# Attention scores and GLA state products on all 128 rows and columns of TensorE

## The chip, the cores and the metric

The kernel runs on one core of a Trainium2 chip. A core has TensorE (PE in the profile: matrix products into PSUM, with a load of the stationary operand, PEld, for each), VectorE (DVE), ScalarE (ACT), GpSimd (POOL) and SyncE (SP), and 16 DMA engines. The metric is device time of one launch in microseconds (us). The kernel before takes 2801.77 us, median of three runs (2800.35 to 2802.33).

## The reference, cut to what matters

One step of a hybrid encoder layer for a prompt of 2048 tokens and a sample of 32. `h = RMSNorm(x)` goes through one in-projection; its columns feed four groups (pooling, chunk-band attention, gated DeltaNet, GLA), an out-projection, a residual, and a squared-ReLU MLP. The two groups that the change touches:

```python
# (B) attention, 4 heads of 64, own chunk of 64 tokens and the 8 before it
s = einsum('bnqhd,bnkhd->bnhqk', qc, kband) * (DH_B ** -0.5) + bias
p = softmax(where(kpos >= 0, s, NEG_INF));  o = einsum('bnhqk,bnkhd->bnqhd', p, vband)

# (D) GLA, 4 heads, key width 32, value width 64; a step for each chunk of 64 tokens
G = cumsum(gc, axis=2)
att = einsum('bhik,bhjk,bhijk->bhij', qc, kc, where(incl, exp(G_i - G_j), 0))
o = einsum('bhik,bhkv->bhiv', qc * exp(G), S) + einsum('bhij,bhjv->bhiv', att, vc)
S = exp(G_last) * S + einsum('bhjk,bhjv->bhkv', kc * exp(G_last - G), vc)
```

## The kernel before, in words

The program has two phases. Phase 1 (about the first 1,250 us) runs the in-projection of four blocks of 512 tokens, then the out-projection, as "filling" products (tiles `g`, and `s` where they borrow that tile), and beside them three lanes: attention, DeltaNet and GLA. `drive` emits one step of filling and then as many steps of each lane as its pace allows; a scheduler that keeps a timeline then sets the final order on every engine's queue. So narrow products of the lanes stand between long runs of filling products on one in-order TensorE queue. Phase 2 is the MLP (tiles `u`, `d`) and has no lanes.

Precision: most large products are done in three parts with a number split in an upper and a lower part (`split`, type F32R: one record in the trace for each product). Products of plain F32 appear as two records each, `x64` for 32 products.

Attention scores. For each head (64 features) `split` in `attn` puts q's upper part on the head's own half of the 128 partitions (`me`) and q's lower part on the other half, k's upper part on both halves (tile `qk`), and k's lower part in tile `kl`, on the half `me` alone. A query tile of 128 tokens needs, for each of two PSUM banks, `qk` x `qk` over 128 rows (both parts of q times k's upper part) and then `qk[me]` x `kl` over 64 rows. These are the rows `s<-qk` and `s<-kl,qk`, at most 320 columns each.

GLA. A tile has 128 tokens, two chunks of 64. `gla_factors` makes on GpSimd `qe` (tile `qeg`, q times e^G) and `kd`; `gla` transposes `kd`, and ScalarE copies it to `kt` (tile `ktg`, line 1221). For each chunk q of the tile, `gla` multiplies that chunk's 64 columns of `qe` by the state S into the chunk's 64 partitions of the output (`l<-Sg,qeg`: 128 rows, 64 columns of the array), and that chunk's 64 partitions of `kt` by v into the state's update (`a<-lvg,ktg`: 64 rows, 128 columns). `l<-lvg,att` and `l<-Qx,Cl` are the other GLA products, over the whole array.

Shapes in the profile: `64*128 64x320` is 64 rows times 128 columns of the array, and a moving operand of 64 partitions by 320. All products carry line 90 or 94, the helper `PT`, so they are told apart by tile names.

The lines that matter: 739 to 754 (`split`), 780 and 781 (the score products), 1178 (`qeg`), 1220 and 1221 (`ktg`), 1250 and 1252 (the two GLA products), and the pools in `phase1`.

Of the kernel before, what the change touches and what calls it, by code (L numbers as in the profile page):

```python
# [8 lines left out]
F32 = mybir.dt.float32  # L9
# [4 lines left out]
ALU = mybir.AluOpType  # L14
# [5 lines left out]
P = 128  # L20
# [4 lines left out]
LAG = 7  # L25
# [13 lines left out]
# columns of the array of small parameters  # L39
# [30 lines left out]
# the pieces of the in-projection: feature-major and token-major; the last is token-major  # L70
# [4 lines left out]
class PT:  # L75
    """A PSUM tile: its matmuls issue in order, and the first into a bank x quadrant clears it."""
# [15 lines left out]
    def tr(self, out, src, n):  # L92
        """out = src transposed, n the partitions of src"""
        return self.order(self.k.nc.tensor.transpose(out, src, self.k.c["ident"][:n, :n]))  # L94
# [16 lines left out]
class K:  # L111
# [14 lines left out]
    # ------------------------------------------------------------------ the order on the tensor engine  # L126
    def pace(self, ins):
        """notes the last product of each lane; a filling product issues behind those of LAG steps ago"""
        if self.lane is not None:
            self.front[self.lane] = ins  # L130
        for b in self.bound if self.lane is None else ():
            self.tc.add_manual_dep(
                ins.ins, b.ins.name,
                mybir.DependencyInfo(mybir.DependencyClass.NoSync, mybir.DependencyReason.DATA),
                reason="pace")
        if self.lane is None:
            self.bound = []

    # ------------------------------------------------------------------ side jobs: each goes on by one step a tick
# [19 lines left out]
    def store(self, dst, src, wait=2, key=None):  # L159
        """a store that is issued when its data should be there"""  # L160
# [8 lines left out]
    def ready(self, *keys):  # L169
        """everything of these kinds has been computed and its stores issued"""  # L170
        return all(k in self.done and not self.todo.get(k) for k in keys)

    # ------------------------------------------------------------------ constants
# [56 lines left out]
    def bias(self):  # L230
        """attention bias, negated: nb[i, h, kj] = -table[h, clip(kj - 512 - i)], +BIG outside the band"""
# [15 lines left out]
    # ------------------------------------------------------------------ helpers  # L247
    def split(self, hi, lo, src, scale=None, eng=None):
        """hi = round(src * scale), lo = src * scale - hi, both exact in 12 bits"""
# [11 lines left out]
    def wdma(self, src, ncols):  # L261
        """weights [128, 8, ncols] as two halves (4 k-tiles each)"""
# [7 lines left out]
    def wload(self, src, ncols, raws=None):  # L270
        """weights as two halves split into hi and lo"""
# [12 lines left out]
    # ------------------------------------------------------------------ norm of a block's x, feature-major  # L284
    def xrows(self, b, u):
        """half u of block b's tokens: two tiles of four k-tiles each"""
        if u == 0:
            xs = [self.ld.tile([P, 4 * 280], F32, name="xt", tag="ld")[:, 0:D] for _ in range(2)]
        else:
            # these go where nothing else is at that time  # L290
# [6 lines left out]
    def xnorm(self, b, xs, n):  # L297
        """x times (mean(x^2) + eps)^-1/2 of its token"""
# [37 lines left out]
    def xsplit(self, xs, o, n, f=None):  # L336
        """times the norm's gain, split, to tokens from o; f: times this before"""
# [12 lines left out]
    def gemm_fm(self, w, ct, hT, b, odd, halves):  # L350
        """[128 columns, tokens of the block]: yields times, then the pieces of the segments"""
# [14 lines left out]
        # the sample's columns go with the second half  # L366
# [21 lines left out]
    def gemm_tm(self, w, hT, o, m, ncols):  # L388
        """[m tokens from o, ncols]"""
# [10 lines left out]
    # ------------------------------------------------------------------ in-projection  # L400
# [5 lines left out]
    def spare(self, b, n):  # L406
        """in the first block, a tile of what the attention takes later"""
# [7 lines left out]
    def spill_fm(self, seg, b, idx, src, n, key):  # L415
        """[128, n] feature-major to the scratch tiles of block b"""
# [8 lines left out]
    def conv(self, b, pieces, n, ct, tail, newtail):  # L425
        """short conv over the columns of the pieces (history in tail), then silu"""
# [18 lines left out]
    def l2(self, seg, b, x, ct, n):  # L445
        """q (ct 0, 1) or k (2, 3): each head's 64 partitions scaled to length one, to scratch"""
# [11 lines left out]
    def silu_tm(self, ps, g, m):  # L458
        """silu(ps) * g, g [128, 64] for each head"""
# [11 lines left out]
    def stage_in(self, b):  # L471
        """all projections of block b (and of the sample, with block 0), what follows them token by token, to scratch"""
# [75 lines left out]
        for z, key in enumerate(order):  # L548
# [25 lines left out]
            if key[0] == "fm":  # L574
# [4 lines left out]
                if z == 0:  # L579
                    # the first half of the tokens goes ahead  # L580
# [18 lines left out]
            else:  # L599
                for seg, n in segs[::-1]:  # L600
                    for i in range(max(1, n // 128)):
# [4 lines left out]
                        if z == last and b + 1 < NBLK and seg == 0:  # L606
                            # the next block's rows, where the tokens of this one are done with
# [32 lines left out]
    # ------------------------------------------------------------------ pooling  # L640
# [36 lines left out]
    # ------------------------------------------------------------------ attention  # L677
    def attn_head(self, n, scores, base, c0, c1, vs, nbv, o, after=None):
        """one head: scores(S) gives q.k of the key columns from c0 to c1 in S, from column base;
        vs: (v, keys, column) in order; o [n, 64] of the result"""  # L680
# [27 lines left out]
    def load_bias(self, h):  # L708
        """nb[i, kj] = -table[h, clip(kj - 512 - i)], +BIG outside the band"""
# [8 lines left out]
    def attn(self, b):  # L718
        """the query tiles of a block, one head after the other"""
# [6 lines left out]
        def loads(h):  # L726
            """raw q and k of a head on both halves of the partitions, its v and its bias"""
# [12 lines left out]
        def split(h, raw):  # L740
            """q: its upper part and, on the other half of the partitions, its lower part; k: the upper part on both; kl: k's lower part"""
            r = h % 2
            me, other = slice(64 * r, 64 * r + 64), slice(64 - 64 * r, 128 - 64 * r)
            H = self.at.tile([P, 1536], F32R, name="qk", tag="qk")
            kl = self.kl
            for z, x in enumerate(raw):
# [4 lines left out]
                rows = me if z else other  # L751
                dst = kl[rows, o - 512:o] if z else h_[rows]
                nc.gpsimd.tensor_tensor(dst, x[rows], h_[rows].bitcast(F32), ALU.subtract)
            return H, kl[me]
# [4 lines left out]
        for h in range(4):  # L759
            raw, v = nxt  # L760
            me = slice(64 * (h % 2), 64 * (h % 2) + 64)
# [8 lines left out]
            for i in range(4):  # L770
# [3 lines left out]
                def scores(S):  # L774
                    # the columns up to 128 * i + 640, cut where a bank ends
                    cut = 128 * i + 320
                    for z, (a, e) in enumerate(((c0, cut), (max(c0, cut), 128 * i + 640))):
                        if a < e:
                            o = S.t[:, 192 + a - 128 * i:192 + e - 128 * i]
                            S.mm(o, 0, P, qk[:, qs], qk[:, 512 + a:512 + e], bank=z)  # L780
                            S.mm(o, 0, P, qk[me, qs], kl[:, a:e], bank=z)
# [45 lines left out]
    # ------------------------------------------------------------------ gated norm and transposition  # L827
    def gated(self, o, gate, n):
        """o: PSUM [n, 256]; gate [n, 256]"""
# [12 lines left out]
    def mix_out(self, o, n, seg, t, kt):  # L842
        """o [n, 256]: k-tiles kt, kt + 1 of the mixed features of tile t"""
# [9 lines left out]
    # ------------------------------------------------------------------ DeltaNet  # L853
    def decay(self, seg, b, z, n):
        """decay and beta of a segment's tiles: g, beta [128, nt, 4]"""
# [16 lines left out]
        # a chunk's g in two parts, the upper on its own half of the partitions and the lower on the other  # L872
# [9 lines left out]
    def delta_pre(self, b):  # L882
        """what the chunks of a block (and, with block 0, of the sample) need besides the state, to scratch: q e^G, k e^G
        (feature-major); k e^(G_last - G), v, masked q.k and (I + A)^-1 (transposed; tokens on partitions)"""
# [3 lines left out]
        # a tile each: segment, tile, index in the block, tokens, tokens of a chunk, chunks  # L888
# [32 lines left out]
        for z, (seg, T, t, m, cs, nch) in enumerate(ent):  # L921
            chs = [slice(64 * q, 64 * q + cs) for q in range(nch)]
            g, be, egl = (x[:, t] for x in self.gb[seg][b][0:3])
            # cumulated decay, per token and as rows over all partitions
# [11 lines left out]
            # dec[j, h, i] = exp(G_i - G_j) for i >= j  # L936
# [3 lines left out]
            # exp(G) over the feature-major tokens  # L940
# [15 lines left out]
            # k and v with tokens on partitions; q.k and k.k within chunks, [j, i]  # L956
# [21 lines left out]
            # the 32 x 32 diagonal blocks of A, gathered  # L978
# [817 lines left out]
```

## Time and profile before

| what | value |
|---|---|
| three runs, median (lowest, highest) | 2801.77 us (2800.35, 2802.33) |
| the profiled execution: its span | 2802.3 us |
| PE busy | 2730.2 us, 97% |
| PEld busy | 2348.8 us, 84% |
| DVE busy | 1647.4 us, 59% |
| ACT busy | 930.2 us, 33% |
| POOL busy | 619.3 us, 22% |
| chain that ended last | PE 86%, DVE 6%, DMA 3%, ACT 2% |

PE's busy time is that of records which overlap and whose ends are modelled: a product's own duration (about 0.4 us for 320 columns) is longer than the time until the next one can start. What a product costs the queue is the distance from its start to the next start, and that is read from the timeline. Engines other than PE are read as a share of a stretch. PEclk is the clock that TensorE was granted, 1.00 for 2.4 GHz and 0.50 for 1.2 GHz.

### The profile page before, as it was taken

How to read it: one execution, taken by the hardware profiler on the slowest of the kernel's cores; microseconds unless marked ns; L12 is line 12 of the kernel's file. 1: busy time of each engine (PE TensorE's matmuls, PEld its weight loads, DVE VectorE, ACT ScalarE, POOL GpSimd, SP SyncE). 2: the span in 40 equal slices, each digit the busy share in tenths (PEclk: the TensorE clock that was granted, in tenths of full speed). 3: DMA queues.
4: the chain of work that ended last, by engine and by line, in shares of the span. 5: the costliest groups of instructions: out<-in, count | busy, mean ns of one | idle time of the engine just before them, and what ended most of it. 6: DMA issues, size and time to landing. Idle time of an engine off the chain costs nothing.

```text
span 2802.3 us, 41267 instructions
## 1 busy us (share of the span) xinstructions
PE 2730.2 (97%) x16044; PEld 2348.8 (84%) x16044; DVE 1647.4 (59%) x3081; ACT 930.2 (33%) x1742; POOL 619.3 (22%) x866
## 2 busy tenths in 40 slices
PE   7999999999999999989999999999999999999998
PEld 6887777778777777768888888888799999999997
DVE  6577689767876965465444444454754545454444
ACT  6536534543464343243212121232331212121212
POOL 3534555554455442230000000010300000000001
PEclk9998999999999999999999999999999999999999
DMA  5654454354545465257111110131341111111111
GB/s 175 188 152 143 133 158 152 123 152 126 161 134 170 122 204 161 89 178 239 43 48 53 38 60 31 60 108 46 107 167 38 53 38 54 38 53 39 53 31 62
DMA packets 195267, 292.88 MB, mean 105 GB/s; under 512 B 41344, under 2 KB 129680, under 8 KB 195072
## 3 DMA queue, kind: packets, MB, share of 16 engines
q1 hardware_dynamic: 123344, 231.58, 26.8%
q10 hardware_dynamic: 71664, 58.59, 6.3%
q8 instruction: 126, 2.06, 0.3%
q14 instruction: 69, 0.57, 0.1%
q0 software_dynamic: 64, 0.08, 0.0%
HBM read 227.67 MB, written 63.64 MB: 104 GB/s over the span
## 4 chain that ended last, share of the span: by engine, by line
PE 86%; DVE 6%; DMA 3%; ACT 2%; issue 1%; POOL 1%; SPq 0%; ACTq 0%; DVEq 0%; POOLq 0%
PE d L90 28%; PE u L90 26%; PE g L90 20%; PE s L90 5%; PE a L90 3%; PE l L90 3%; PE s L94 1%; PE a L94 1%; DVE wt L253 1%; DVE h2T L256 1%; DVE X L1001 1%; DVE tp L1000 0%; ACT wt L252 0%; DVE acc L1656 0%; DMA tmd<-sg 0%
## 5 line engine op out<-in xcount | busy, mean ns | idle before, releaser
L1656 DVE TENSOR_TENSOR acc<-acc,d 128x352 f32<-128x352 f32 (+1 forms) x616 | 360.8, 589 | 500.4 <-PE d L90 495.4
L90 PE MATMUL u<-h2T,wt 128*128 128x352 f32 (+1 forms) x2536 | 634.5, 352 | 0.0
L90 PE MATMUL d<-u,wt 128*128 128x352 f32 (+1 forms) x2576 | 624.7, 352 | 3.9 <-DVE acc L1656 3.9
L90 PE MATMUL g<-hT,wt 128*128 128x512 f32 (+2 forms) x2544 | 541.6, 362 | 14.4 <-ACT hT L252 6.0
L90 PEld LDWEIGHTS d<-u,wt 128*128 128x128 f32 x2576 | 455.5, 188 | 52.3 <-DVE acc L1656 7.0
L90 PEld LDWEIGHTS u<-h2T,wt 128*128 128x128 f32 x2536 | 451.8, 188 | 45.3 <-issue 0.5
L90 PEld LDWEIGHTS g<-hT,wt 128*128 128x128 f32 x2544 | 411.7, 194 | 90.2 <-issue 16.8
L90 PE MATMUL u<-h2T,wx 128*128 128x352 f32 (+1 forms) x1304 | 390.2, 350 | 0.0
L90 PE MATMUL d<-u,wx 128*128 128x352 f32 (+1 forms) x1264 | 356.7, 351 | 0.3 <-DVE acc L1656 0.3
L1637 ACT ACTIVATE rr<-u 128x352 f32<-128x352 f32 (+1 forms) x160 | 81.2, 516 | 636.8 <-PE u L90 596.1
L90 PEld LDWEIGHTS u<-h2T,wx 128*128 128x128 f32 x1304 | 238.9, 188 | 22.4
L90 PEld LDWEIGHTS d<-u,wx 128*128 128x128 f32 x1264 | 228.5, 188 | 22.2 <-DVE acc L1656 0.8
L90 PE MATMUL g<-wt,hT 128*128 128x256 f32 (+3 forms) x1632 | 242.6, 298 | 3.6 <-DVE sg L464 3.1
L90 PEld LDWEIGHTS g<-wt,hT 128*128 128x128 f32 (+1 forms) x1632 | 212.4, 189 | 19.0 <-issue 9.2
L253 DVE TENSOR_TENSOR wt<-ldt,wt 128x1024 fp32r<-128x1024 f32 (+1 forms) x120 | 160.0, 1333 | 67.1 <-ACT wt L252 66.4
L1671 POOL TENSOR_TENSOR fs<-fs,sq 128x352 f32<-128x352 f32 (+1 forms) x15 | 17.0, 1134 | 767.3 <-ACT sq L1669 767.3
L252 ACT CAST wt<-ldt 128x1024 fp32r<-128x1024 f32 (+1 forms) x120 | 126.0, 1050 | 125.2 <-PE g L90 81.2
L1554 POOL TENSOR_TENSOR nss<-nss,xp 128x1024 f32<-128x1024 f32 (+1 forms) x8 | 19.5, 2440 | 627.7 <-ACT xp L1552 604.3
L252 ACT CAST wt<-wur 128x1024 fp32r<-128x1024 f32 x85 | 87.7, 1045 | 185.1 <-PE u L90 101.0
L1638 DVE SCALAR_TENSOR_TENSOR rr<-u,rr 128x352 f32<-128x352 f32 (+1 forms) x160 | 92.7, 587 | 79.6 <-ACT rr L1637 79.0
L252 ACT CAST u<-rr 128x352 fp32r<-128x352 f32 (+1 forms) x160 | 82.9, 539 | 115.6 <-PE d L90 59.4
L253 DVE TENSOR_TENSOR u<-rr,u 128x352 fp32r<-128x352 f32 (+1 forms) x160 | 95.3, 617 | 23.1 <-ACT u L252 19.6
(324 smaller groups left out, 3343.0 us busy)
## 6 DMA issues: line engine op xcount, KB each, us to landing
wur<-w_up SPq DMA_DIRECT2D x64, 512.0 KB, 3.5
wur<-w_down SPq DMA_DIRECT2D x64, 512.0 KB, 3.5
ldt<-w_fm SPq DMA_DIRECT2D x56, 512.0 KB, 4.2
ldt<-w_o SPq DMA_DIRECT2D x32, 512.0 KB, 5.1
ldt<-w_tm SPq DMA_DIRECT2D x24, 512.0 KB, 3.9
fmd<-sg ACTq DMA_DIRECT2D x46, 256.0 KB, 2.6
qkr<-fmd SPq DMA_DIRECT2D x88, 128.0 KB, 3.6
xp<-x2d SPq DMA_DIRECT2D x16, 528.0 KB, 3.7
```

Of the source, the lines that this page charges most:

```text
L90: return self.order(self.k.nc.tensor.matmul(out, lhsT, rhs, start=not have, stop=True, skip_group_check=True))
L94: return self.order(self.k.nc.tensor.transpose(out, src, self.k.c["ident"][:n, :n]))
L252: nc.scalar.copy(hi, src)
L253: (eng or nc.vector).tensor_tensor(lo, src, hi.bitcast(F32), ALU.subtract)
L256: nc.vector.scalar_tensor_tensor(lo, src, scale, hi.bitcast(F32), ALU.mult, ALU.subtract)
L1001: v.tensor_tensor(X[:, w:32, 0:w], X[:, w:32, 0:w], tv, ALU.subtract)
L1554: (nc.gpsimd if i % 2 else nc.vector).tensor_tensor(ss, ss, x, ALU.add)
L1637: nc.scalar.activation(rr[:, :cw], ps.t[:, :cw], AF.Relu)
L1638: nc.vector.scalar_tensor_tensor(rr[:, :cw], ps.t[:, :cw], 0.0, rr[:, :cw], ALU.max, ALU.mult)
L1656: nc.vector.tensor_tensor(x, x, ps.t[:, :cw], ALU.add)
L1671: (nc.vector if i % 2 else nc.gpsimd).tensor_tensor(fs[i % 2], fs[i % 2], sq, ALU.add)
```

## The change

Three things, all in phase 1.

1. `split` computes k's lower part on all 128 partitions instead of the half `me`, and the second score product multiplies the whole `qk` by the whole `kl`: 128 rows instead of 64. (It then also adds q's lower part times k's lower part.)
2. `qe` of a tile is written into one of two fixed tiles `qez` of 384 columns, the first chunk at columns 0 to 63 and the second at 192 to 255, the rest zero. Each chunk's product with the state uses 128 columns, of which the other chunk's 64 are zero, and is added to all 128 partitions of the output.
3. `kt` becomes a fixed tile `ktz` with two layers, one for each chunk, zero at the other chunk's tokens; ScalarE fills it with two copies of 64 partitions instead of one of 128. Each chunk's update multiplies over 128 rows.

The fixed tiles are zeroed by three GpSimd memsets at the start. The sample's 32 tokens keep their narrow products. The launch also asks for a smaller scratch for software DMA, and comments are dropped, which shifts line numbers.

```diff
-                rows = me if z else other
-                dst = kl[rows, o - 512:o] if z else h_[rows]
+                rows = slice(0, P) if z else other
+                dst = kl[:, o - 512:o] if z else h_[rows]
                 nc.gpsimd.tensor_tensor(dst, x[rows], h_[rows].bitcast(F32), ALU.subtract)
-            return H, kl[me]
+            return H, kl
...
                             S.mm(o, 0, P, qk[:, qs], qk[:, 512 + a:512 + e], bank=z)
-                            S.mm(o, 0, P, qk[me, qs], kl[:, a:e], bank=z)
+                            S.mm(o, 0, P, qk[:, qs], kl[:, a:e], bank=z)
...
-        qe = wk.tile([P, P], F32, name="qeg", tag="qeg", bufs=2)
-        nc.gpsimd.tensor_tensor(qe[:, :n], q, eg[:, :n], ALU.mult)
+        nch = n // cs
+        if nch == 2:
+            self.qn += 1
+            qe = self.qez[self.qn % 2]
+            e4 = qe.rearrange("p (x s) -> p x s", s=192)[:, :, 0:64]
+        else:
+            qe = wk.tile([P, P], F32, name="qeg", tag="qeg")
+            e4 = qe[:, :n].unsqueeze(1)
+        nc.gpsimd.tensor_tensor(e4, q.rearrange("p (x s) -> p x s", s=cs), eg[:, :n].rearrange("p (x s) -> p x s", s=cs), ALU.mult)
...
-            kt = wk.tile([P, P], F32, name="ktg", tag="ktg")
-            nc.scalar.copy(kt[:n], pk.t[:n, 0:128])
+            kt = self.ktz
+            for q in range(nch):
+                ch = slice(64 * q, 64 * q + cs)
+                nc.scalar.copy(kt[ch, q], pk.t[ch, 0:128])
...
-                po.mm(po.t[co:co + cs, 0:256], co, cs, qe[:, co:co + cs], S)
+                po.mm(po.t[:n, 0:256], 0, n, qe[:, P * q:P * q + n], S)
                 pu = self.aux()
-                pu.mm(pu.t[:, 0:256], 0, P, kt[co:co + cs], vt[co:co + cs])
+                pu.mm(pu.t[:, 0:256], 0, P, kt[:n, q], vt[:n])
...
+            self.qez = [self.gk.tile([P, 3 * P], F32, name="qez", tag=f"qez{z}") for z in range(2)]
+            self.ktz = self.gk.tile([P, 2, P], F32, name="ktz", tag="ktz")
+            self.qn = 0
+            for x in self.qez:
+                nc.gpsimd.memset(x, 0.0)
+            nc.gpsimd.memset(self.ktz, 0.0)
...
-    nc = bacc.Bacc("TRN2", target_bir_lowering=False, num_devices=1)
+    nc = bacc.Bacc("TRN2", target_bir_lowering=False, num_devices=1, dynamic_dma_scratch_size=4096)
```

The order on the queues. TensorE's queue around a score tile and the first chunk of a GLA tile (the tenth of 16), before; in the trace this is the stretch from 599.5 to 606 us. `d` is DeltaNet, `g` filling, `a<-c,sqo` and `a<-c,lc` transpositions over the whole array.

```order
L90 MATMUL s_6793<-qk 128x320
L90 MATMUL s_6793<-kl,qk 128x320
L90 MATMUL s_6793<-qk 128x320
L90 MATMUL s_6793<-kl,qk 128x320
L90 MATMUL d_6857<-X,ltk 64x64
L90 MATMUL g_6956<-hT,wt 128x512 x3
L90 MATMUL l_7018<-lvg,att 128x64 x4
L90 MATMUL l_7018<-Sg,qeg 64x256
L90 MATMUL g_6956<-hT,wt 128x512 x2
L94 MATMUL a_6845<-c,sqo 128x128 x2
L90 MATMUL g_7099<-hT,wt 128x512 x6
L94 MATMUL a_6886<-c,lc 128x128 x2
```

The same score tile and GLA tile on TensorE's queue of the changed kernel.

```order
L90 MATMUL s_6792<-qk 128x320
L90 MATMUL s_6792<-kl,qk 128x320
L90 MATMUL s_6792<-qk 128x320
L90 MATMUL s_6792<-kl,qk 128x320
L90 MATMUL d_6856<-X,ltk 64x64 x4
L90 MATMUL g_7097<-hT,wt 128x512 x6
L94 MATMUL a_6844<-c,sqo 128x128 x2
L90 MATMUL l_7016<-lvg,att 128x64 x4
L90 MATMUL l_7016<-Sg,qez 128x256
L94 MATMUL a_6885<-c,lc 128x128 x2
L90 MATMUL a_6885<-lc 64x2x64 x4
```

The four score products stand as they stood; `Sg,qez` now writes 128 partitions, and around it a few filling products and transpositions have changed places.

ScalarE's queue at the copy of `kt`, before. `qk` is a cast of the attention split, `st` a norm, `wt` a weight's split.

```order
L750 CAST qk<-qkr 128x512
L836 ACTIVATE st<-st,epst 128x4
L252 CAST wt<-ldt 128x1024
L165 DMA tmd_127<-sg 128x256
L1221 COPY ktg<-a_7804 128x128
L837 ACTIVATE st<-st 128x4
L697 COPY pT<-s_7789 128x640
```

The same place on ScalarE's queue of the changed kernel.

```order
L750 CAST qk<-qkr 128x512 x2
L835 ACTIVATE st<-st,epst 128x4
L252 CAST wt<-ldt 128x1024
L165 DMA tmd_133<-sg 128x256
L1230 COPY ktz<-a_7801 64x128 x2
L836 ACTIVATE st<-st 128x4
L697 COPY pT<-s_7786 128x640
```

One copy of 128 partitions has become two of 64, in the same place; behind them stand the norm and the copy of the probabilities (`pT`) as before.

## Rows read from the trace of the kernel before

**Rows 1.** The page: the chain that ended last, by engine.
```profile
PE 86%; DVE 6%; DMA 3%; ACT 2%; issue 1%; POOL 1%; SPq 0%; ACTq 0%; DVEq 0%; POOLq 0%
```

**Rows 2.** Stretches: length; busy PE, PEld, DVE, ACT, POOL; PEclk, DMA share, GB/s.
```profile
200.00:1230.00 1030.00, 1008.08 (x6559) 793.67 (x6558) 733.42 (x1613) 469.55 (x961) 468.13 (x696) 0.98 0.49 148
200.00:300.00 100.00, 91.02 (x638) 72.16 (x637) 74.22 (x161) 57.93 (x128) 44.12 (x78) 0.91 0.45 139
300.00:400.00 100.00, 100.00 (x675) 80.52 (x674) 69.24 (x177) 44.48 (x103) 59.28 (x94) 1.00 0.54 167
400.00:500.00 100.00, 95.51 (x715) 76.80 (x713) 90.53 (x199) 44.42 (x99) 48.11 (x67) 0.97 0.46 142
1160.00:1180.00 20.00, 20.00 (x91) 13.72 (x89) 6.08 (x13) 2.78 (x6) 2.33 (x3) 0.72 0.13 40
1230.00:2802.00 1572.00, 1544.44 (x8193) 1394.84 (x8191) 783.59 (x1177) 364.35 (x553) 67.18 (x34) 0.99 0.21 68
```

**Rows 3.** Groups of PE instructions by shape, us 0 to 1230.
```profile
L90 PE MATMUL l<-Qx,Cl 128*128 128x256 f32 x192 | 52.3, 394 | 1.5 <-DVE att L1237 1.4
L90 PE MATMUL s<-kl,qk 64*128 64x320 f32 x104 | 42.8, 411 | 0.0
L90 PE MATMUL a<-lvg,ktg 64*128 64x256 f32 x64 | 23.0, 440 | 0.0
L90 PE MATMUL l<-Sg,qeg 128*64 128x256 f32 x64 | 21.0, 420 | 0.0
```

**Rows 4.** Instructions of tile kl: count, duration in ns, first and last start.
```profile
L90 PE MATMUL s<-kl,qk x120: 294/410/633, 209.1 to 1193.8; 64*128 64x320 f32 x104, 64*128 64x128 f32 x4, 64*128 64x256 f32 x4, 64*128 64x64 f32 x4
```

**Rows 5.** Timeline of PE at a score tile: start, us until the last end.
```profile
901.10 0.31 PE L90 MATMUL s<-qk 128*128 128x320 f32 x1
901.34 0.41 PE L90 MATMUL s<-kl,qk 64*128 64x320 f32 x1
901.68 0.42 PE L90 MATMUL s<-qk 128*128 128x320 f32 x1
902.03 0.41 PE L90 MATMUL s<-kl,qk 64*128 64x320 f32 x1
902.37 0.44 PE L94 MATMUL a<-c,lc 128*128 128x128 f32 x2
```

**Rows 6.** Timeline of PE at filling products of 256 columns.
```profile
910.10 1.93 PE L90 MATMUL g<-wt,hT 128*128 128x256 f32 x15
911.86 0.33 PE L90 MATMUL s<-vh,pT 128*128 128x64 f32 x2
```

**Rows 7.** Timeline of PE at filling products of 512 columns.
```profile
842.89 2.95 PE L90 MATMUL g<-hT,wt 128*128 128x512 f32 x12
845.68 0.71 PE L94 MATMUL s<-c,s 128*128 128x128 f32 x5
```

**Rows 8.** Timeline of PE at a state update of GLA, filling products around it.
```profile
618.77 1.32 PE L90 MATMUL g<-hT,wt 128*128 128x512 f32 x5
620.02 0.70 PE L90 MATMUL a<-lvg,ktg 64*128 64x256 f32 x2
620.65 1.66 PE L90 MATMUL g<-hT,wt 128*128 128x512 f32 x6
622.14 0.38 PE L94 MATMUL a<-c,lc 128*128 128x128 f32 x2
```

**Rows 9.** Timeline of PE at a product with GLA's state.
```profile
602.76 0.65 PE L90 MATMUL l<-Sg,qeg 128*64 128x256 f32 x2
603.34 0.74 PE L90 MATMUL g<-hT,wt 128*128 128x512 f32 x2
603.91 0.38 PE L94 MATMUL a<-c,sqo 128*128 128x128 f32 x2
```

**Rows 10.** Timeline of PE at whole-array GLA products of 256 columns.
```profile
366.01 1.02 PE L90 MATMUL l<-Qx,Cl 128*128 128x256 f32 x4
366.87 0.55 PE L90 MATMUL s<-vh,pT 128*128 128x64 f32 x4
```

**Rows 11.** Groups on POOL and ACT by shape.
```profile
L753 POOL TENSOR_TENSOR kl<-qkr,qk 64x512 fp32r<-64x512 f32 x28 | 38.7, 1396 | 6.6 <-ACT qk L750 5.5
L442 POOL TENSOR_TENSOR sg<-sg 128x512 f32<-128x512 f32 x18 | 25.5, 1414 | 42.1 <-ACT sg L441 24.7 <-DMA lqke<-fmd 8.1 <-DVE oa L702 7.2
L1221 ACT COPY ktg<-a 128x128 f32<-128x128 f32 x16 | 4.2, 265 | 5.2 <-PE a L90 5.2
```

**Rows 12.** POOL's memsets, and its first wait in the timeline.
```profile
L993 POOL MEMSET X<- 128x1024 f32 x1 | 1.0, 961 | 0.2 <-DMA tmd<-kvq 0.2
...
12.95 0.33 POOL L430 COPY sgs<-pv 128x3 f32<-128x3 f32 x1 [9.83 <-DMA pv<-par]
```

More of the change, by code (lines that the diff above doesn't have):

```diff
@@ L742, in split @@
             r = h % 2
-            me, other = slice(64 * r, 64 * r + 64), slice(64 - 64 * r, 128 - 64 * r)
+            other = slice(64 - 64 * r, 128 - 64 * r)
             H = self.at.tile([P, 1536], F32R, name="qk", tag="qk")
@@ L760, in attn @@
             raw, v = nxt
-            me = slice(64 * (h % 2), 64 * (h % 2) + 64)
             if h < 3:
```

## The prediction

> **What bounds the kernel now.** I read the chain that ended last first: TensorE holds 86% of it, and no other engine more than 6% [rows 1]. Then the stretches. The change touches only products that issue from 209 us on, the last `kl` product at 1194 [rows 4] and the GLA ones in the same stretch, so I take 200 to 1230 us: there PE is busy 1008 of 1030 us, DVE 733, ACT 470, POOL 468 [rows 2]. TensorE leaves 22 us idle in 1030, so its queue sets the pace. The rest, 1230 to 2802 us, is MLP and holds none of these products; I leave it as it is. Last, the timeline of TensorE, because a busy sum of overlapping records hides what a product costs. There the reader is to look at the distances between starts.
>
> **What a narrow product costs.** First the price of a product among its like. Fifteen filling products of 256 columns take 911.86 - 910.10 = 1.76 us, 0.117 each [rows 6]; twelve of 512 take 845.68 - 842.89 = 2.79, 0.2325 each [rows 7]. Between them 320 columns are worth 0.117 + 64 x (0.2325 - 0.117) / 256 = 0.146 us. Now a score tile [rows 5]: from the first `kl` product's start (901.34) to the second's (902.03), in which one `kl` and one `qk` product of 320 columns run, 0.69 us pass where two at 0.146 would take 0.29. So 0.40 us go each time the queue passes from 128 rows to 64 and back, 0.2 for each passing: the next weight load and product start only when the product ahead is through, and then the load itself stands open. In the run of [rows 6] no such gap stands, though each product there loads weights too. What costs is the change of the part of the array that is used.
>
> **The change part by part.**
>
> *Scores.* 120 `kl` products [rows 4], of which 104 have 320 columns [rows 3]; the 16 narrower ones pass the same two borders. 120 x 0.40 = 48 us. Going through the trace's queue, 11 of them are followed by a product that uses part of the array anyway, and there one border stays: 11 x 0.2 = 2. Saved: 46 us. Nothing is added on TensorE: the columns stay 320.
>
> *GLA's state update.* From 618.77 to 622.14 stand eleven filling products and one update (two records): 3.37 - 11 x 0.2325 = 0.81 us [rows 8]. The same two records over the whole array, of 256 columns, cost 2 x (366.87 - 366.01) / 4 = 0.43 [rows 10]. Saved 0.38; 64 records of 64 rows [rows 3] are 32 updates: 12.2 us.
>
> *GLA's product with the state.* From 602.76 to 603.91: 1.15 us with two filling products of 0.2325, so 0.685, [rows 9], and the border ahead of it some 0.09, read from [rows 8] (620.02 - 618.77 - 5 x 0.2325). 0.775 - 0.43 = 0.345; 32 of them [rows 3]: 11 us. Of the 128 borders of both kinds, 28 lie against other narrow products (DeltaNet's `d`, `a<-un`, 32 x 32 ones), where a border stays, and 5 are shared by two of these groups: 33 x 0.2 = 6.6 us to take off. GLA: 12.2 + 11 - 6.6 = 16.6 us.
>
> Together 63 us. The order of the changed kernel gives nearly the same: neighbours on TensorE's queue that use different parts of the array fall from 819 to 490, and 329 x 0.2 is 66. I take 64 as what TensorE's queue gets shorter by.
>
> *Work on other engines.* The subtraction for `kl` covers 128 partitions instead of 64. POOL took 1396 ns for 64 x 512 and 1414 for 128 x 512 in an operation of the same kind [rows 11], so I price it at nothing; by partitions it would be 28 x 1.4 = 39 us more on POOL, which has 562 idle in that stretch [rows 2]. The second copy of `kt` adds 16 copies of about 265 ns [rows 11], bounds 2 to 5 us in all, on ACT, which is idle 560; behind it stand a norm and the copy of the probabilities, each then some 0.27 us later, and the product that reads `kt` comes only after three further steps of its lane. If that cover were gone it would cost 16 x 0.27 = 4.3 us. `qe` keeps its 128 columns in one instruction. Three memsets of 1024 columns in all are about 1 us on POOL, as one of 1024 columns took 961 ns, and POOL sits idle 9.83 us at that place waiting for the small parameters [rows 12]: hidden. The smaller scratch concerns only the two loads that POOL issues at the start; nothing shows a price for it, so 0, with 0 to 3 us in the range.
>
> *What comes through.* With TensorE's work shorter by 64 in 1030 us, something else is late more often: the softmax (scores, DVE, ACT, back to TensorE) and DeltaNet's chain keep their length. DVE is at 71% over the stretch and at 90.5% in 400 to 500 us [rows 2], which a stretch shorter by 6 us still holds. The idle 22 us are 2%; I let them grow by 8, an estimate, and keep both ends: by none, or by 40, where DVE's and the chains' waits eat most of the gain. 64 - 8 = 56. The profiled span is 2802.3 us and the runs' median 2801.8, so nothing lies around the span that would have to be added: 2802 - 56 = 2746 us.
>
> **The rivals.**
>
> *The side engines take it back.* Every product with a result to wait for is now reached earlier, and DVE, at 74 to 90% in 200 to 300 and 400 to 500 us, answers no sooner. For it: those two rows. Against: 100 of 100 us busy on TensorE in 300 to 400 us with DVE at 69%. Gain 64 - 34 = 30: 2772 us.
>
> *More than the sum.* In 1160 to 1180 us PE is busy all the time, yet its clock is 0.72 [rows 2], at 1.2 GHz for more than half of it, and the products there are the narrow ones. Over the whole stretch a mean clock of 0.98 is some 41 us at 1.2 GHz, which costs about 20. If fewer borders keep the clock up, 66 + 12: 2724 us.
>
> *Open weight loads.* The new products could pay for their loads: a product on the same rows as the one ahead would have to wait for it with its load, about 0.1 us (the border behind the update: 622.14 - 620.65 - 6 x 0.2325 = 0.095 [rows 8]). Then each passing gives back half, 32 us: 2770. Against: 0.117 us for 256 columns in [rows 6] leaves no room for an open load, and all those products use the same rows. The Trainium skill says this in "TensorE: Matmul & The Clock Gate", Part 3: a weight load overlaps a running product only where the row groups differ. The trace does not agree for whole-array products.
>
> *Nothing.* The gaps come from something else in the score tile (the bank, the tile `kl`), and stay: 2802. Against: the same 0.2 us stands at GLA's and DeltaNet's borders, in other banks.
>
> *Slower.* TensorE, sooner done, waits more often, and its clock falls after waits. In 200 to 300 us, where PE idles 9 us, the clock is 0.91: 18 us at 1.2 GHz, twice the idle time [rows 2]. To eat 64 us of gain the time at 1.2 GHz would have to grow from 41 to about 170 us, a sixth of the stretch; at 200 it would be 2802 - 64 + (200 - 41) / 2 = 2818 us. It decides from some 65 us of added idle time on. Against: TensorE now idles 22 us in all.
>
> **How the numbers follow.** Chances: forecast 0.62 (its own range 2735 to 2760), side engines 0.16, more than the sum 0.13, open loads 0.04, nothing 0.02, slower 0.03. The range 2726 to 2777 takes in the two rivals beside the forecast. A difference of 0.2% (5.6 us) is about what a measurement of this kernel can tell from no change: faster by more than that 0.95, within it 0.02, slower 0.03.
>
> **What would show it.** In the changed kernel's timeline the four score products should start about 0.15 us apart; a GLA update among filling products should take 0.43 us and leave no gap behind it. `kl` and `qk` products' distances of 0.34 would make the first step wrong, distances of 0.25 would be open loads. PE's idle time between 200 us and the end of phase 1 should stay under about 40 us and the clock at 0.97 or more; if phase 1 ends less than 40 us earlier with the products at 0.15, the gain went into waits on DVE. The MLP should last as long as before; the subtraction for `kl` should still take about 1.4 us.

## The result, and the profile after

The changed kernel takes 2766.56 us (median of 4 runs, 2760.96 to 2771.29), beside 2802.05 (4 runs, 2800.35 to 2807.47) for the kernel before on the same chip: ratio 0.9878, 95% interval 0.9863 to 0.9892. That is 35.5 us faster where 56 were forecast; the time lies in the range 2726 to 2777, 21 us above the value. The direction and the main mechanism were right. Two terms of the sum were mis-sized: the scores, at 46 us of TensorE's queue, took off about 36, and "What comes through" let 8 us be lost in waits where the traces show 16 to 19. One execution of a kernel tried below (`LAG` = 5) took 6907.22 us and is the one that was traced, so it is left out of that kernel's time and its trace is not used.

First the page's head and the chain by engine, of the changed kernel.

```profile
span 2759.2 us, 41285 instructions
PE 2670.6 (97%) x16044; PEld 2344.7 (85%) x16044; DVE 1652.4 (60%) x3081; ACT 933.2 (34%) x1758; POOL 620.6 (22%) x869
PE 82%; DVE 9%; DMA 4%; issue 2%; ACT 2%; POOL 1%; SPq 0%; ACTq 0%; DVEq 0%; POOLq 0%
```

Against [rows 1], TensorE's share of the chain falls from 86 to 82% and DVE's rises from 6 to 9%. PE's idle time over the span was 2802.3 less 2730.2 busy before (72.1 us) and is 2759.2 - 2670.6 = 88.6 now. So the span lost 43.1 us, PE's busy time 59.6, and 16.5 us of that came back as waits.

The score tile in the timeline of PE (start, us until the last end, then the instruction), changed kernel; it answers to [rows 5].

```profile
619.12 0.31 PE L90 MATMUL s<-kl,qk 128*128 128x320 f32 x1
619.27 0.30 PE L90 MATMUL s<-qk 128*128 128x320 f32 x1
619.41 0.31 PE L90 MATMUL s<-kl,qk 128*128 128x320 f32 x1
619.56 0.75 PE L90 MATMUL g<-wt,hT 128*128 128x256 f32 x5
```

The starts stand 0.14 to 0.15 us apart, where a pair took 0.69 us before. The state update, same view, answers to [rows 8].

```profile
703.37 0.86 PE L90 MATMUL g<-hT,wt 128*128 128x512 f32 x3
704.06 0.59 PE L90 MATMUL a<-lvg,ktz 128*128 128x256 f32 x2
704.49 0.71 PE L94 MATMUL s<-c,s 128*128 128x128 f32 x5
```

704.49 - 704.06 = 0.43 us for the two records, and the three filling products ahead take their plain 0.69: nothing is lost on either side. Both prices of a product came out to a hundredth of a us.

Now the stretches (length; busy PE, PEld, DVE, ACT, POOL; granted clock, DMA share, GB/s), changed kernel, beside [rows 2].

```profile
200.00:1230.00 1030.00, 979.17 (x6690) 814.82 (x6691) 769.53 (x1635) 489.52 (x993) 484.54 (x701) 0.97 0.51 155
200.00:300.00 100.00, 88.75 (x638) 72.44 (x639) 73.59 (x160) 57.97 (x131) 43.02 (x80) 0.90 0.45 139
300.00:400.00 100.00, 99.78 (x694) 83.27 (x693) 72.08 (x185) 45.97 (x105) 61.78 (x95) 1.00 0.54 166
400.00:500.00 100.00, 90.93 (x733) 78.78 (x734) 91.84 (x199) 48.30 (x109) 47.83 (x66) 0.97 0.47 142
```

From 200 to 1230 us PE now idles 51 us where it idled 22. Phase 1 ends earlier, so these 1030 us now hold some 43 us of work that used to come later, with its waits; over the same work, from 200 us to the first MLP product, idle time grows from 34 to 53 us, and over all of phase 1 from 56 to 73. The stretch 400 to 500 us, where DVE was already at 90.5%, leaves PE idle for 9.1 us (4.5 before) with DVE at 91.8%. The waits of PE in the first 1330 us name the releasers (total us, times, longest; the two long waits that stood before too, for the constants and for `hT`, are left out).

```profile
PE l L90 <- DVE att L1246: 5.1, 5, 1.8
PE a L90 <- ACT sg L449: 5.0, 4, 3.3
...
PE s L94 <- ACT s L687: 4.5, 8, 0.9
PE s L90 <- DVE oa L702: 3.7, 2, 3.2
PE s L90 <- ACT pT L697: 3.4, 3, 2.9
```

No new wait is longer than 3.3 us: GLA's masked product (`att`) waited 1.4 us before [rows 3] and waits 5.1 in five pieces. The growth is many small waits on DVE and ACT, not one.

Phase 1 (up to the first MLP product) ends at 1272.1 us instead of 1315.2, and from there to the end it is 1487.1 us in both. The profiled execution is the fastest of the four, 5.6 us under their median; by the runs' medians the loss is 64 - 35.5, some 29 us, by the two profiled ones 64 - 43 = 21.

### The profile page after: what moved, and what is told of

The parts are those of the page before. It is cut to its first block, busy times and chain, and to the rows that moved or that the text cites. A ratio compares the mean times of both kernels' runs of the same rounds, so it can differ in the third digit from the quotient of the medians.

```text
span 2759.2 us, 41285 instructions
## 1 busy us (share of the span) xinstructions
PE 2670.6 (97%) x16044; PEld 2344.7 (85%) x16044; DVE 1652.4 (60%) x3081; ACT 933.2 (34%) x1758; POOL 620.6 (22%) x869
## 4 chain that ended last, share of the span: by engine, by line
PE 82%; DVE 9%; DMA 4%; issue 2%; ACT 2%; POOL 1%; SPq 0%; ACTq 0%; DVEq 0%; POOLq 0%
PE d L90 28%; PE u L90 26%; PE g L90 17%; PE s L90 4%; PE a L90 3%; PE l L90 2%; DVE wt L253 1%; PE s L94 1%; DVE tp L999 1%; DMA x2d<-sg 1%; DVE X L1000 1%; DVE h2T L256 1%; PE a L94 1%; DMA ldt<-w_o 1%; DVE hT L256 0%
## 5 line engine op out<-in xcount | busy, mean ns | idle before, releaser
L90 PE MATMUL g<-hT,wt 128*128 128x512 f32 (+2 forms) x2544 | 539.9, 361 | 15.6 <-ACT hT L252 4.7
L253 DVE TENSOR_TENSOR wt<-ldt,wt 128x1024 fp32r<-128x1024 f32 (+1 forms) x120 | 163.2, 1360 | 65.0 <-ACT wt L252 64.4
```

The lines of the kernel that those rows point to most:

```text
L90: return self.order(self.k.nc.tensor.matmul(out, lhsT, rhs, start=not have, stop=True, skip_group_check=True))
L253: (eng or nc.vector).tensor_tensor(lo, src, hi.bitcast(F32), ALU.subtract)
```

## The experiments

Three explanations of the missing 20 to 30 us stood against each other: the border's price is less than 0.2 us on the average; DVE, back to back in places, doesn't answer sooner; or the scheduled order of the changed kernel happens to let less through. The first two turn out to hold for the scores. All ratios are to the kernel before on the same chip (its medians 2800.55, 2801.64 and 2800.35 us). "Borders" are neighbours on TensorE's queue that use different parts of the array, counted in each kernel's order: 819 before, 490 in the changed kernel.

**The score part alone** (the GLA part left as before). 591 borders, so 228 x 0.2 = 45.6 us.

```diff
-                dst = kl[rows, o - 512:o] if z else h_[rows]
+                dst = kl[:, o - 512:o] if z else h_[rows]
...
-                            S.mm(o, 0, P, qk[me, qs], kl[:, a:e], bank=z)
+                            S.mm(o, 0, P, qk[:, qs], kl[:, a:e], bank=z)
```

> The kernel before with the score part of the change alone; every queue keeps its order row for row. The scores' term of the sum was 46 us of TensorE time. Theory A (the borders are gone in full, side engines take a share of what TensorE gains): score products 0.147 us apart, PE idle grows by some 10 to 20 us, time 25 to 36 us under before (2766 to 2777). Theory B (what went missing is the price of the new order that the scheduler made of the GLA part): with the order unchanged nearly all comes through, 40 to 46 us under before (2756 to 2762).

Measured 2769.95 us (0.9887, 0.9874 to 0.9901): 30.6 us, two thirds of the sum, in theory A's range; the interval overlaps that of the whole change, 0.9863 to 0.9892, so the runs don't show that the GLA part adds anything to it. Every queue holds the same instructions in the same order as before, so no scheduling is in it, and the traces can be laid side by side product by product.

First the price. The distances into and out of the 120 `kl` products are shorter by 36 us in sum, 0.30 us a product, where the sum took 46. The same comparison gives 36 us in two more pairs of kernels with one order (the GLA part alone beside the changed kernel, and less DVE with and without the score part, both below). [rows 5] show the main reason: the first passing of a tile, from 901.10 to 901.34, costs 0.24 - 0.146 = 0.09 us and not 0.2. The tile's four products take 1.27 us there; four at 0.146 take 0.58, so 0.69 us are saved and not 0.80. Ten of the missing 15 us were never there to be saved.

Then the waits. From 600 to 1150 us the lead over the kernel before grows by 25.5 us, 0.36 for each of 71 `kl` products (3 of the 25.5 because the time at 1.2 GHz is shorter there). From 300 to 600 us it does not grow: -1.5, -0.2 and +1.2 us in the three hundreds, with 33 `kl` products that at 0.30 should have brought 10. So the loss also has a place. Two windows of the kernel before, whose columns are those of the stretches above:

```profile
300.00:600.00 300.00, 294.89 (x1987) 236.12 (x1985) 232.55 (x524) 147.13 (x316) 160.36 (x232) 0.99 0.48 146
1150.00:1180.00 30.00, 30.00 (x141) 20.82 (x140) 13.18 (x34) 5.29 (x11) 7.03 (x12) 0.77 0.20 62
```

The same two of the kernel with the score part alone:

```profile
300.00:600.00 300.00, 287.72 (x1982) 237.18 (x1981) 233.06 (x523) 146.77 (x316) 159.54 (x231) 0.97 0.48 146
1150.00:1180.00 30.00, 30.00 (x166) 23.55 (x164) 15.59 (x30) 10.43 (x18) 1.78 (x2) 1.00 0.51 161
```

In the first, as many products are done in the same 300 us. PE idles 7.2 us more (12.3 for 5.1), and the clock is 0.97 for 0.99: 17 us at 1.2 GHz for 7, which cost 5 us. Together that eats the 9 us that the products there gave by their distances. In the second the clock was 0.77 and is 1.00: a stretch of 13.65 us at 1.2 GHz (1157.6 to 1171.2 us) is gone, and half of it, some 6.8 us, is won there.

**The GLA part alone** (the change with the score part taken back). 719 borders: 20 us.

```diff
-                            S.mm(o, 0, P, qk[:, qs], kl[:, a:e], bank=z)
+                            S.mm(o, 0, P, qk[me, qs], kl[:, a:e], bank=z)
```

> The changed kernel with the score part undone; its queues have the changed kernel's order, row for row. The GLA term was 17 us, 20 with the new order's fewer borders. Theory A: 9 to 15 us under before (2787 to 2793). Theory B: the new order costs 20 us, which the GLA term only just pays: 2799 to 2806.

Measured 2793.6 us (0.9973, 0.9962 to 0.9983): 7 us, a third, just outside theory A's range and well under theory B's. PE spends 88.7 us of phase 1 at 1.2 GHz in this trace, 75.1 before. The two parts together, 30.6 + 7, are near the whole change's 35.5, so within the runs' spread the parts add up.

**Both `qk` products, then both `kl` products**, all with their old rows: half of the score borders go, and no operation changes.

```diff
-                    for z, (a, e) in enumerate(((c0, cut), (max(c0, cut), 128 * i + 640))):
+                    for y in range(2):
+                        for z, (a, e) in enumerate(((c0, cut), (max(c0, cut), 128 * i + 640))):
...
+                                if y == 0:
+                                    S.mm(o, 0, P, qk[:, qs], qk[:, 512 + a:512 + e], bank=z)
+                                else:
+                                    S.mm(o, 0, P, qk[me, qs], kl[:, a:e], bank=z)
```

> The kernel before with the four score products of a tile in another order: both qk products, then both kl products of 64 rows. Nothing else moves on DVE and ACT. If what costs is the border between parts of the array, 56 tiles lose two borders each, 56 x 0.4 = 22 us of TensorE time, and the time is 12 to 22 us under before (2780 to 2790); the distance from the first to the second kl product is 0.15 us. If a 64-row product is itself slow, whatever stands ahead of it, the distance stays 0.34 and the time within 3 us of before.

Measured 2783.83 us (0.9939, 0.9926 to 0.9951): 16.7 us of the 22 that 110 fewer borders give. A score tile of this kernel in PE's timeline:

```profile
890.44 0.46 PE L90 MATMUL s<-qk 128*128 128x320 f32 x2
890.82 0.56 PE L90 MATMUL s<-kl,qk 64*128 64x320 f32 x2
891.31 0.44 PE L94 MATMUL a<-c,lc 128*128 128x128 f32 x2
```

From the first start to the product behind the tile 0.87 us pass, for 901.10 to 902.37, 1.27, in [rows 5]: 0.40 for two borders, with the 64-row products untouched. So alternating between parts of the array costs 0.2 us a change. But the other half of the expectation failed: the two `kl` products take 891.31 - 890.82 = 0.49 us, 0.245 each, where 0.15 was expected for a product without a border ahead. Over the 47 tiles of four products of 320 columns in this trace the second `kl` product starts 0.25 us behind the first (median), and with all 128 rows, in the kernel with the score part alone, products of 320 columns start 0.147 apart. So 64 rows cost 0.1 us a product even behind their like, and both explanations hold in part. The Trainium skill's "TensorEngine Tiling (Array Packing)", Key Properties, says that changing the tiling mode drains TensorE; the trace agrees that a change costs time, 0.2 us where products alternate, and shows the 0.1 us beside it.

**GLA's products over the whole array without the zeroed copies**, with the score part: 502 borders, 63 us, and none of the change's extra copies.

```diff
-                po.mm(po.t[co:co + cs, 0:256], co, cs, qe[:, co:co + cs], S)
+                po.mm(po.t[:n, 0:256], 0, n, qe[:, :n], S)
...
-                pu.mm(pu.t[:, 0:256], 0, P, kt[co:co + cs], vt[co:co + cs])
+                pu.mm(pu.t[:, 0:256], 0, P, kt[:n], vt[:n])
```

> The kernel before with the score part, and with GLA's two products over the whole array but without zeros in their operands, so GLA's state and output take in the other chunk's tokens: that part of the computation is changed. No second ScalarE copy, no memsets; the scheduler makes a third order of it. TensorE loses the same borders as in the changed kernel, about 64 us. Theory A: as the changed kernel, 2760 to 2772. Theory B: the order decides, and a third order differs from the changed kernel by 8 us or more, to either side.

Measured 2778.46 us (0.9919, 0.9906 to 0.9932): 22 us, less than the change itself, as theory B said. So the gain is lost without the second `kt` copy and the strided `qe` too; they aren't needed to explain it. The other difference is that the scheduler made another order of it, and the kernel is 12 us slower than the change: order had to be tried by itself.

**DVE's load, without and with the score part.** DeltaNet's forward substitution is a row of 2 x 31 dependent DVE instructions to a block. Between 350 and 520 us they take 32 of DVE's 143.5 busy us, and from 400 to 460 us DVE is busy 57.5 of 60. These two kernels leave out 30 of the 31 steps, and the scheduler makes another order of what is left.

```diff
-            v.tensor_tensor(tv, bc(B[:, w:32, q:w], [P, r, w]), bc(X[:, q:w, 0:w], [P, r, w]), ALU.mult)
-            v.tensor_tensor(X[:, w:32, 0:w], X[:, w:32, 0:w], tv, ALU.subtract)
+            if q == 30:
+                v.tensor_tensor(tv, bc(B[:, w:32, q:w], [P, r, w]), bc(X[:, q:w, 0:w], [P, r, w]), ALU.mult)
+                v.tensor_tensor(X[:, w:32, 0:w], X[:, w:32, 0:w], tv, ALU.subtract)
```

> The kernel before with 30 of the 31 steps of the forward substitution left out (DeltaNet's inverses are not computed rightly), 60 of 62 DVE instructions for each of four blocks, some 111 us of DVE time before 1230 us. It is the base for the next kernel, whose queues have the same order row for row. Theory A1 (in 200 to 520 us DVE, at 84 to 90%, decides): this alone is 10 us or more under the kernel before. Theory A2 (TensorE's queue decides everywhere, and what went missing of the gain went into the clock): within 6 us of before.

> The same left out, with the score part of the change. With DVE's load taken away the score part should give its whole term by theory A1: 40 to 46 us under the kernel less_dve, against 31 with the load. By theory A2 the difference stays 28 to 34.

Measured 2786.04 us (0.9949, 0.9934 to 0.9963) without the score part and 2749.32 (0.9814, 0.9797 to 0.983) with it; the two have the same order on every queue. The first is 15.6 us under the kernel before, as theory A1 said. The score part now brings 36.7 us, where it brought 30.6 under the full load; with runs that spread over 10 us each, the times alone don't tell these two apart, but the traces do. In the stretch 300 to 600 us the lead grows by 1.8, 3.9 and 3.2 us, where it did not grow at all. The window 350 to 520 us under the full load, the kernel before and then the kernel with the score part:

```profile
350.00:520.00 170.00, 165.45 (x1186) 133.33 (x1185) 143.54 (x315) 74.26 (x164) 89.78 (x131) 0.98 0.50 154
350.00:520.00 170.00, 159.33 (x1157) 132.36 (x1157) 143.66 (x313) 71.54 (x160) 88.56 (x129) 0.95 0.49 151
```

and with the substitution left out, again without and with the score part:

```profile
350.00:520.00 170.00, 167.71 (x1203) 135.08 (x1202) 115.63 (x258) 79.94 (x170) 78.81 (x128) 0.98 0.49 150
350.00:520.00 170.00, 167.44 (x1238) 138.12 (x1237) 124.03 (x265) 82.98 (x177) 84.31 (x135) 0.98 0.52 158
```

Under the full load the score part lets PE's idle time there grow from 4.6 to 10.7 us; without the substitution it goes from 2.3 to 2.6. So what the score part loses to waits there goes with this substitution. Whether by its load on DVE, by the length of its chain, or by the order that goes with it, these kernels don't tell apart. 36.7 lies between what the two theories gave, and it is all that the products had to give: 36 us by their distances. That settles the score part: of the 46 us, 10 were not there, and some 5, net, went into waits.

**Work moved from DVE to POOL**, in the changed kernel: half of the weight splits' subtractions of block 1, then of blocks 1 to 3.

```diff
-            self.split(hi, lo, raw)
+            self.split(hi, lo, raw, eng=self.nc.gpsimd if q and self.blk == 1 else None)
```

> The changed kernel with the second half of each weight's lower part computed on GpSimd instead of DVE while block 1 is projected: 11 subtractions of 1.3 us leave DVE. Theory A1: 5 to 12 us under the changed kernel (2755 to 2762). Theory A2: no change within 4 us. A rival of its own: POOL needs about twice as long for it and weights come late, slower by 3 us or more.

> The same in blocks 1 to 3: 33 subtractions leave DVE for GpSimd. From 520 us on the score part came through nearly whole, so by theory A1 blocks 2 and 3 add little: within 5 us of pool_b1. If DVE held TensorE everywhere, another 8 to 15 us.

Measured 2778.4 us (0.9919, 0.9907 to 0.9932) and 2802.37 (1.0001, 0.9991 to 1.0011): 12 and 36 us slower than the change. The first is what its own rival said; the second, 24 us above the first, is in neither range. The moved subtraction by line, in the kernel with block 1 moved (count, busy us, mean ns, idle before):

```profile
L254 POOL TENSOR_TENSOR wt<-ldt,wt 128x1024 fp32r<-128x1024 f32 (+1 forms) x11 | 26.5, 2411 | 12.0 <-ACT wt L253 12.0
```

That is 2411 ns on POOL for 1360 on DVE. And the window 350 to 520 us of the same kernel:

```profile
350.00:520.00 170.00, 158.07 (x1196) 133.92 (x1195) 145.12 (x317) 74.58 (x167) 101.86 (x140) 0.97 0.50 153
```

DVE is as busy as in the changed kernel (145.9 of 170 us there), though subtractions are gone from it, and each moved one takes 1.05 us longer. The busy row of the page of the kernel with blocks 1 to 3 moved shows the same for the whole run:

```profile
PE 2692.0 (96%) x16044; PEld 2356.2 (84%) x16044; DVE 1658.1 (59%) x3048; ACT 934.4 (33%) x1758; POOL 682.8 (24%) x902
```

Thirty-three instructions are gone from DVE, some 45 us at 1360 ns, and yet DVE is busy 1658.1 us for 1652.4. So its other instructions took some 50 us longer while POOL had more to do: the update of GLA's state (`Sg`, 33 times 128x256), for one, took 814 ns on the mean for 570 in the changed kernel. Moving the work did not lighten DVE, so these two kernels say nothing about whether DVE's load decides. They show only that the move costs more than it frees, through the longer subtraction, through DVE's slower instructions, or both.

**The order.** `LAG` sets how many steps a filling product is held behind each lane; it is 7.

```diff
-LAG = 7
+LAG = 8
```

> The changed kernel with LAG = 5 instead of 7: a filling product is bound to the lanes' products of five steps ago, so the scheduler makes another order of the same instructions. 482 borders on TensorE's queue instead of 490. Theory A (DVE's load alone keeps the rest back): the time is the changed kernel's within 5 us, 2762 to 2772, since neither the borders nor DVE's work differ. Theory C (how long the lanes' steps have, which the order sets, decides how much of the 64 us comes through): shorter room for them, 5 to 20 us slower than the changed kernel.

> The same with LAG = 6 (493 borders). Theory A: 2762 to 2772. Theory C: 0 to 10 us slower than the changed kernel.

> The same with LAG = 8 (509 borders, 4 us more of TensorE time). Theory A: 2766 to 2776. Theory C: more room for the lanes' steps, 0 to 10 us faster than the changed kernel in spite of the borders.

> The same with LAG = 10 (494 borders). Theory A: 2762 to 2772. Theory C: 5 to 15 us faster than the changed kernel, 2752 to 2762, and the fastest of all.

Measured 2781.49 us for 5 (0.9933, 0.9919 to 0.9946), 2768.11 for 6 (0.9884, 0.987 to 0.9897), 2792.4 for 8 (0.9967, 0.9954 to 0.9979) and 2790.15 for 10 (0.9967, 0.9955 to 0.9979). The same products with 482 to 509 borders give times 26 us apart. Theory A holds for 6 alone. No setting beats 7, and no kernel here that does the whole work beats the changed one, though 6 and the score part alone lie within its interval. That the order moves the time is shown; theory C, that a longer lag lets more through, held for 5 and 6 and was wrong for 8 and 10. At 8 the softmax is late, in PE's waits of the first 1330 us:

```profile
PE s L94 <- ACT s L687: 17.1, 10, 5.9
```

That is 17.1 us for 4.5 at 7.

**One account of all traces.** From each profiled execution: the borders; the sum of what lies over 0.3 us between successive PE starts more than 0.6 apart, in phase 1; the time at 1.2 GHz in phase 1, which costs half its length. The account is (819 - borders) x 0.2, less the growth of the gaps over 52.6, less half the growth of the 1.2 GHz time over 75.1.

| kernel | borders | gaps, us | at 1.2 GHz, us | account, us | phase 1 earlier by, us |
|---|---|---|---|---|---|
| before | 819 | 52.6 | 75.1 | 0 | 0 |
| changed | 490 | 69.9 | 71.7 | 50 | 43.1 |
| score part alone | 591 | 65.2 | 71.7 | 35 | 30.8 |
| GLA part alone | 719 | 62.7 | 88.7 | 3 | 5.2 |
| `qk` twice, `kl` twice | 709 | 56.7 | 61.4 | 25 | 23.6 |
| whole array, no zeros | 502 | 75.2 | 81.9 | 37 | 32.3 |
| less DVE | 830 | 46.7 | 44.4 | 19 | 20.2 |
| less DVE, score part | 604 | 48.2 | 47.8 | 61 | 54.8 |
| block 1 to POOL | 497 | 78.9 | 81.9 | 35 | 28.3 |
| blocks 1 to 3 to POOL | 506 | 92.5 | 109.2 | 6 | 0.7 |
| LAG 6 | 493 | 72.6 | 81.9 | 42 | 34.3 |
| LAG 8 | 509 | 85.2 | 112.6 | 11 | 11.1 |
| LAG 10 | 494 | 83.4 | 105.8 | 19 | 18.2 |

The limits of 0.3 and 0.6 us are choices; no number was fitted to the times. The account meets the traces to within 8 us, mostly above them: 0.2 us is too much for a border, as the score part's 228 took off 36 us and not 45.6. Among kernels with nearly the same borders (490 to 509) what sets them apart is the waits, and the 1.2 GHz time that mostly goes with them: it is longest where the gaps are (`LAG` 8 and 10, blocks 1 to 3 on POOL) and shortest where they are fewest.

## Why the prediction was right or wrong

*What a narrow product costs: right in kind, too high for the scores.* Starts stand 0.14 to 0.15 us apart, and a state update takes 0.43. The term for the scores was 46 us and measured 36. The prediction took 0.40 from the distance of one `kl` product to the next and gave it to all 120; the first passing of each tile, 0.09 us in the same [rows 5], was priced at 0.2. For GLA's state product the prediction did use 0.09 for the border ahead. "What costs is the change of the part of the array" is half of it: the paired kernel saves 0.40 us a tile by two changes fewer, but a 64-row product costs 0.1 us even behind another. The two ways of counting, 63 from rows and 66 from the order, agreed because both used 0.2; PE's busy time fell by 59.6 us, 0.18 a border.

*Work on other engines: right.* Groups by line of the changed kernel, beside [rows 11] and [rows 3]:

```profile
L753 POOL TENSOR_TENSOR kl<-qkr,qk 128x512 fp32r<-128x512 f32 x28 | 37.2, 1342 | 3.2 <-ACT qk L750 2.7
L90 PE MATMUL l<-Sg,qez 128*128 128x256 f32 x64 | 20.5, 405 | 0.1
L90 PE MATMUL a<-lvg,ktz 128*128 128x256 f32 x64 | 20.4, 402 | 0.0
```

The subtraction over 128 partitions takes 1342 ns on the mean, no more than the 1396 that 64 took; no wait for the copies of `kt` stands in the list of PE's waits. The smaller scratch was not tried alone.

*What comes through: the mechanism right, the size wrong.* The step took PE's idle 22 us and let them grow by 8, "with both ends: by none, or by 40". They grew by 19 over the same work (from 34 to 53 us, from 200 us to the end of phase 1) and by 29 in the fixed window 200 to 1230 us (22 to 51), between the two ends. The estimate read a stretch's mean: DVE at 90.5% in 400 to 500 us looked like room for 6 us. But a mean hides that DVE is busy 57.5 of 60 us from 400 to 460. The score part got nothing for its 33 `kl` products in 300 to 600 us, and without the substitution it got nearly all. The sign that the prediction set, idle time over about 40 us from 200 us to the end of phase 1, came at 53; the kernel before had 34 by that measure. Its other sign did not: phase 1 ended 43 us earlier in the profiled execution, not less than 40.

*The rivals.* "The side engines take it back", 2772 us, describes what happened better than the forecast did (2766.56), though by half: the price of the scores, the order of work and the clock have their part. "More than the sum" was right on one place, the 1.2 GHz stretch at 1160 us that went, and wrong on the whole, since other waits brought as much 1.2 GHz time back (75.1 and 71.7 us). Open weight loads are out for the new products: at 0.145 us a product none is open. The rule in the Trainium skill's "TensorE: Matmul & The Clock Gate", Part 3, that loads overlap only across row groups, does not hold for these whole-array products at 0.145 us. "Nothing" is out. "Slower" described a force that is real (`LAG` 8 and blocks 1 to 3 on POOL give back 26 and 36 us, with more waits and more time at 1.2 GHz), but the idle time that came with the change, 19 us, was less than half of the 65 us from which it decides.

*What stays open.* The GLA part's missing 13 us are in the account as gaps and clock, but no run removes them one by one: each edit that moves work also makes another order. How the substitution delays TensorE, by load or by the length of its chain, is open too, and so is why a 64-row product costs 0.1 us behind another.

## What to carry to other kernels

Look at the distances between the starts of products, not at their durations: a product of 64 rows or 64 columns between whole-array ones cost 0.3 to 0.4 us more here. Computing over the whole array, with zeros where they are needed, takes that away, and merely putting like products side by side takes away about half for the scores (16.7 us for another order of four products). Read the distances over a whole group from its first start to the next product, not one pair in its middle: that was worth 10 of 46 us. Then look for the stretches where a side engine runs back to back for longer than the bound engine's queue can wait, and count no gain there: of 64 us, 35 came through. Before work is moved to another engine, see whether the first one is freed by it: 33 instructions left DVE and it was as busy as before. And try the scheduler's own setting beside any such change, since the same products in another order moved the time by 26 us, nearly as much as the change.

## What the runs showed that I had not expected

- The time at 1.2 GHz in phase 1 mostly goes with the waits: 44 us where the gaps sum to 47, 113 where they sum to 85. It does not always: with the score part alone the gaps grew by 12.6 us and the 1.2 GHz time fell by 3.4, one long stretch having gone.
- The changed kernel's runs spread over 10.3 us (2760.96 to 2771.29) and their mean granted clock falls with them from 0.986 to 0.984; the kernel before spread over 7.1 beside it, and over 12.5 in a set of 17 runs.
- POOL took 2411 to 2445 ns for the subtraction of 128 x 1024 that DVE does in 1360.
